# GpSimd for two of the four weight sums of gate and up's seven-product units, and a fourth such unit in ten groups

## The chip, the core and the metric

The kernel runs on one core of a Trainium2 chip. The core has five engines with queues of their own that run side by side and meet at semaphores: TensorE (PE in the profile) multiplies matrices, VectorE (DVE) and ScalarE (ACT) work element by element, GpSimd (POOL) can do that too and here mostly starts transfers, and SyncE (SP) only starts transfers. Each engine takes its own instructions strictly in order. TensorE writes its products to PSUM; all other tiles lie in SBUF. The metric is the time of one execution in microseconds; the median of several runs counts.

## What is computed

One layer of an encoder on 256 rows of 2048 columns, in float32: four mixers side by side, cross attention, and a gated MLP. Only the MLP is touched:

```python
def swiglu(h, w_gate_up, w_down):
    gate, up = jnp.split(h @ w_gate_up, 2, axis=-1)
    return (jax.nn.silu(gate) * up) @ w_down
...
        x = x + swiglu(rms_norm(x, norm_g[l, 2]), w_gate_up[l], w_down[l])
    return rms_norm(x, final_norm_g)
```

`w_gate_up` is 2048 x 11264, `w_down` 5632 x 2048.

## The kernel before

**Products of split numbers.** TensorE multiplies in a rounded format (`fp32r`). To keep float32's accuracy each operand is split into a high part (the number, rounded) and a low part (what is left). One product of 128 rows by 128 columns by 512 columns then takes three matmuls: high times high, high times low, low times high (`part`, L493 to L498). For weights the split is made in the kernel: ScalarE casts a piece of a slab to `wh` (L156), and VectorE subtracts, `wl = raw - wh` (L157).

**The stream of weights.** All weights come in the order of use from one array `W`, in slabs of 128 x 2048 (1 MB each). `Stream.raw` starts a slab's load on SP's queue (L136) as soon as one of its three buffers is free; in gate and up a fourth buffer serves every fourth slab. `Stream.make` splits the next piece into a pair `wh`, `wl`; in gate and up there are five such pairs of buffers, so the splitting engines can be at most five pieces ahead of TensorE. A pair is free again when TensorE has used it.

**Gate and up.** `Block.gate_up` goes through 11 groups `j` of 512 columns of gate and the same 512 columns of up. A group has eight slabs `i`; slab `i` holds rows 2i and 2i+1 (in tiles of 128) of both column blocks, four blocks of 128 x 512. The 256 rows of the activations are two halves, so a slab is a product of 2 x 2 blocks with 2 x 2 blocks:

- A plain slab takes eight products. It has two pieces of 1024 columns, each of which serves four products.
- A seven-product unit forms sums of blocks and takes seven products (Strassen's scheme in Winograd's form). `sevens(j)` says which slabs are units: 5 in group 0, and 1, 3 and 5 in groups 1 to 10. The sums of the activations are the same for all groups and are formed once, by `left()`, in group 0.

A unit's four weight blocks lie in the slab as b11, b12, b22, b21. `make` goes through it in four parts. Part 0 splits b11 alone (512 columns), and then one instruction of 1024 columns overwrites b11 and b12 by b11 - b12 and b22 - b12. Part 1 splits b22 and b21 as they are, and then two instructions of 512 columns each overwrite them: b22 becomes b22 + (b11 - b12), and b21 becomes b21 minus that. Part 2 splits the first two sums, part 3 the last two. Part 0 serves one product, the other three parts two each. `keep` fixes the order of these instructions on each engine as it is written.

After a group `combine` puts the unit products together, `finish` adds the plain ones, applies SiLU and the product, and `store_turned` transposes the result in blocks of 32 on VectorE and writes it to `hidden` in memory with eight transfers a group from GpSimd's queue. `fetch` reads parts of `hidden` back into `tmp` (L941), for the first sixteen tiles while gate and up still run, for the rest in down. `turn` writes the residual, transposed, to memory and reads it back (L1077, L1081), also on GpSimd's queue, spread over the first groups.

**Down** follows with the same stream and some units of its own (slabs from `DOWN` on). It works on the transposed `hidden`.

Of the kernel before, what the change touches and what calls it, by code (L numbers as in the profile page):

```python
# [18 lines left out]
ALU = mybir.AluOpType  # L19
# [3 lines left out]
P = 128  # L23
# [28 lines left out]

def sevens(j):

    return (1, 3, 5) if j else (5,)


FORMED = 6
# [20 lines left out]
DOWN = GU // 16 + 16 * DFF // 1024  # L79
# [6 lines left out]
def seven(slab):  # L86

    j, i = divmod(slab - GU // 16, 8)
    return slab in UNITS if slab >= DOWN else j >= 0 and i in sevens(j)
# [22 lines left out]
class Stream:  # L112
# [48 lines left out]
    def make(self):  # L161

        nc, (slab, part) = self.nc, self.todo
        n = 16 * slab + 8 * part
        if n >= NBLK - HELD:
            parts = [(self.places.pop(0)) for _ in range(2)]
            r = self.raw(slab)[:, part * 1024:part * 1024 + 1024]
            for a, (wh, wl) in zip((0, 512), parts):
                nc.scalar.copy(wh, r[:, a:a + 512])
                nc.vector.tensor_tensor(out=wl, in0=r[:, a:a + 512], in1=wh.bitcast(F32), op=ALU.subtract)  # L170
            self.bg.dve(1024, 2)
            self.items.append((None, parts))
            self.todo = (slab + part, 1 - part)
            return True
        pool = self.free(slab)
        if pool is None:
            return False
        raw = self.raw(slab)
        at = 48 if any(a <= n < b for a, b in ROWS) else 8
        r = raw[:, part % 2 * 1024:part % 2 * 1024 + 1024]  # L180
        if not seven(slab):
            mark = len(nc.cur_bb.bb.instructions)
            self.split(pool, at, r, [0, 256, 512, 1024] if n == 0 else [0, 512, 1024] if n == 8 else [0, 1024])
            if DOWN <= slab < DOWN + 2 * AHEAD:
                self.keep(mark)
            self.todo = (slab + part, 1 - part)
            return True
        mark = len(nc.cur_bb.bb.instructions)
        op = lambda out, a, b, what=ALU.subtract: nc.vector.tensor_tensor(out=out, in0=a, in1=b, op=what)  # L189
        self.split(pool, at, r, [0, 512] if part == 0 else [0, 1024])  # L190
        b11, b12, b22, b21 = (raw[:, a:a + 512] for a in range(0, 2048, 512))
        if part == 0:
            blk = raw.rearrange("p (b c) -> p b c", b=4)
            op(r.rearrange("p (b c) -> p b c", b=2), blk[:, 0:3:2, :], blk[:, 1:2, :].to_broadcast([P, 2, 512]))
            self.bg.dve(1024)
        elif part == 1:
            op(b22, b22, b11, ALU.add)
            op(b21, b21, b22)
            self.bg.dve(1024, 2)
        self.keep(mark)  # L200
        self.todo = (slab + part // 3, (part + 1) % 4)
        return True
# [87 lines left out]
class Block:  # L290
# [226 lines left out]
                    self.bg.poll()  # L517
        return ps

    def store_turned(self, to, u, src, keep=False):  # L520

        nc = self.nc
        self.bg.dve(src.shape[1])
        mark = self.mark()
        nc.vector.transpose(u, src)  # L525
        if keep:
            self.keep_place(mark)
        to = to.rearrange("(b f) t -> f b t", f=32)
        for a in range(4):
            nc.gpsimd.dma_start(to[:, :, 32 * a:32 * a + 32],  # L530
                                u[32 * a:32 * a + 32, :].rearrange("f (b t) -> f b t", t=32))


# [238 lines left out]
    def attention(self):  # L772
        tc, nc, act, st = self.tc, self.nc, self.act, self.st
        with tc.tile_pool(name="atp", bufs=1) as atp, tc.tile_pool(name="kp", bufs=1) as kp, \
# [24 lines left out]
            def load_kv():  # L799
# [12 lines left out]
                for _ in range(5):  # L812
                    fetch()
# [118 lines left out]
    def fetch(self, f, ks, ahead, pause, form=None):  # L932

        m = {}
        for n in range(len(ks) + ahead):
            if n < len(ks):
                k = ks[n]
                while len(self.stored) <= k // 4:
                    yield
                m[k] = self.tmp()  # L940
                self.nc.gpsimd.dma_start(m[k], self.ff[k * P:(k + 1) * P, :])  # L941
            if n >= ahead:
                i = ks[n - ahead]
                if i >= PLAIN:
                    if i % 2:
                        form(i - 1, m.pop(i - 1), m.pop(i))
                        self.have += 2
                        yield 3.0
                    continue
                mark = self.mark()  # L950
                self.split(f[i], m.pop(i))
                self.keep_place(mark)
                self.have += 1
                yield pause

    def gate_up(self, sw, gp, f):

        nc, st = self.nc, self.st
# [6 lines left out]

        def left():

            for i in (5, 1, 3):
                t = [self.tmp() for _ in range(2)]
                for x, k in zip(t, (2 * i, 2 * i + 1)):  # L970
                    nc.scalar.activation(x, self.resk(k), AF.Copy, scale=self.gvec(V_NG + 32, k))
                (a11, a21), (a12, a22) = ((x[:, 0:P], x[:, P:R]) for x in t)
                s = gp.tile([P, 512], F32, name="u", tag="u", bufs=2)
                s1, s2, s3, s4 = (s[:, a:a + P] for a in range(0, 512, P))
                self.stt(s1, a21, -1.0, a22, ALU.mult, ALU.subtract)
                self.stt(s2, s1, -1.0, a11, ALU.mult, ALU.subtract)
                self.tt(s3, a11, a21, ALU.subtract)
                self.tt(s4, a12, s2, ALU.subtract)
                yield
                h, l = sums[i] = [sw.tile([P, 512], F32R, name=f"s{x}{i}") for x in "hl"]  # L980
                self.split2(h, l, s)
                yield
# [26 lines left out]
        def finish(j, cs, s):  # L1009

            for r in range(2):
                self.tt(s[r][0], cs[r][0], s[r][0], ALU.add)
                nc.scalar.activation(s[r][0], s[r][0], AF.Silu, scale=box["col"][:, r:r + 1])
                yield SOON
            for r in range(2):
                g, h = s[r]
                self.tt(h, cs[r][1], h, ALU.add)
                yield SOON
            for r in range(2):
                g, h = s[r]  # L1020
                u = gp.tile([P, 512], F32, name="u", tag="u", bufs=2)
                self.stt(h, h, box["col"][:, r:r + 1], g, ALU.mult, ALU.mult)
                yield SOON
                self.store_turned(self.ff[j * 512:(j + 1) * 512, r * P:(r + 1) * P], u, h)
                yield SOON
            self.stored.append(j)

        ready = [self.late, self.bg.add(norm())]
        forms = self.bg.add(left())
        turned = self.bg.add(self.turn())  # L1030
        early = end = None
        for j in range(DFF // 512):
# [5 lines left out]
            for i in range(8):  # L1038
# [18 lines left out]
                for k in (2 * i, 2 * i + 1):  # L1057
                    for c in range(2):
                        wh, wl = st.take("w_gate_up", k, cols[c], 4)
                        for r in range(2):  # L1060
                            self.part_rows(cs[r][c], r, self.h3[k], wh, wl, k == 0, k == KT - 1)
                            self.bg.poll()
            self.bg.drain(last)
            end = self.bg.add(finish(j, cs, s))
        return end, turned, early

    def turn(self):

        nc = self.nc
        to = self.xr.rearrange("(b t) f -> t b f", t=32)  # L1070
        for i in range(16):
            u = self.tmp()
            self.bg.dve(R)
            nc.vector.transpose(u, self.resk(i))
            for a in range(4):
                c = i * P + 32 * a
                nc.gpsimd.dma_start(to[:, :, c:c + 32], u[32 * a:32 * a + 32, :].rearrange("t (b f) -> t b f", f=32))  # L1077
            yield 4.0
        for c in range(4):
            for r in range(2):  # L1080
                nc.gpsimd.dma_start(self.half(c, r), self.xr[r * P:(r + 1) * P, c * 512:(c + 1) * 512])  # L1081
            yield

    def half(self, c, r):
# [4 lines left out]
class Down:  # L1089
# [8 lines left out]
    def form(self, k, m1, m2):  # L1098


        b = self.b
        (a11, a21), (a12, a22) = ((x[:, 0:P], x[:, P:R]) for x in (m1, m2))
        s = self.sd.tile([P, 512], F32, name="e", tag="e", bufs=4)[:, 0:384]
        s2, s3, s4 = (s[:, a:a + P] for a in range(0, 384, P))
        b.tt(s3, a11, a21, ALU.subtract)
        b.stt(a21, a21, -1.0, a22, ALU.mult, ALU.subtract)
        b.stt(s2, a21, -1.0, a11, ALU.mult, ALU.subtract)
        b.tt(s4, a12, s2, ALU.subtract)
        b.split(self.f[k], m1)
        b.split(self.f[k + 1], m2)  # L1110
        t = self.sd.tile([P, 768], F32R, name=f"s{k}")
        b.split2(t[:, 0:384], t[:, 384:768], s)
        self.forms[k] = t
# [765 lines left out]
```

## Time and profile before

| | us |
|---|---|
| median of three runs (1453.46 to 1453.94) | 1453.75 |
| the run that was profiled | 1454.31 |
| its span, first to last instruction | 1452.4 |
| gate and up on TensorE, first to last matmul (749.6 to 1207.6) | 458.0 |
| sums of weight blocks on VectorE (L189), x129, first and last start | 768.7 and 1388.2 |
| loads of weights L136, x259, issue time of one on SP | 0.33 |
| stores of hidden L530, x88, issue time of one on GpSimd | 0.65 |

The granted clock of TensorE was 0.998. The page gives busy times of each engine and, in forty slices of the span, busy tenths. A row of instructions names line, engine, operation and tiles, then busy time, count or mean, and behind the bar the idle time in front of them with the engine that ended it. In a view in order of time a row gives the start, the length, the instruction and, in brackets, the idle time before it and what ended that. A row of a stretch gives each engine's busy time in it. The rows themselves stand in the prediction where they are used.

### The profile page before, as it was taken

The numbers are of one execution on the slowest core, as the hardware profiler recorded it, in microseconds if no ns is written. First come the engines' busy times: TensorE is split into PE (matmuls) and PEld (weight loads), VectorE is DVE, ScalarE is ACT, GpSimd is POOL, SyncE is SP. The second block draws the span as 40 slices with busy tenths as digits, with TensorE's granted clock in tenths as the row PEclk, the third lists the DMA queues.
The fourth block names the chain that finished last, engine by engine and source line by source line (L and its number), as shares of the span: only waits on it lengthen the run. The fifth ranks groups of instructions, "written<-read, shape, count | busy, mean of one in ns | idle before, by whom it ended". The sixth has DMA issues, their size and how long they took to land.

```text
span 1452.4 us, 19765 instructions
## 1 busy us (share of the span) xinstructions
PE 1439.1 (99%) x7231; PEld 1217.8 (84%) x7231; DVE 1192.3 (82%) x1750; ACT 844.1 (58%) x1254; POOL 172.2 (12%) x294
## 2 busy tenths in 40 slices
PE   9999999999999999999999999999999999999997
PEld 8888888898899888888888888888888888788886
DVE  6587768778868767877778999999999997988875
ACT  6565655466656646765565555555655564655554
POOL 0220100000000001100003334112111112100000
PEclk9999999999999999999999999999999999999999
DMA  9985654454535656555555767666667656655654
GB/s 352 339 289 197 220 193 168 152 187 156 195 129 206 215 179 224 172 170 195 178 205 205 277 234 243 220 209 237 233 220 250 221 200 220 214 184 199 225 203 146
DMA packets 57394, 307.17 MB, mean 211 GB/s; under 512 B 9773, under 2 KB 11470, under 8 KB 25680
## 3 DMA queue, kind: packets, MB, share of 16 engines
q1 hardware_dynamic: 45920, 281.11, 54.9%
q0 software_dynamic: 10944, 24.14, 5.4%
q8 instruction: 57, 0.93, 0.3%
q10 hardware_dynamic: 432, 0.66, 0.1%
q14 instruction: 41, 0.34, 0.1%
HBM read 291.71 MB, written 14.16 MB: 211 GB/s over the span
## 4 chain that ended last, share of the span: by engine, by line
PE 94%; DVE 2%; issue 2%; ACT 1%; DMA 1%; POOL 1%; SPq 0%; DVEq 0%; POOLq 0%; ACTq 0%
PE pg L444 19%; PE pg L496 13%; PE pg L497 13%; PE pg L495 13%; PE pg L445 10%; PE pm L496 6%; PE pm L495 6%; PE pm L497 6%; PE pm L1380 1%; DVE wl L157 1%; PE pg L441 1%; PE pg L442 1%; PE pm L895 1%; PE pm L868 1%; DMA tmp<-hidden 1%
## 5 line engine op out<-in xcount | busy, mean ns | idle before, releaser
L156 ACT CAST wh<-raw 128x1024 fp32r<-128x1024 f32 (+1 forms) x589 | 589.2, 1013 | 466.6 <-PE pg L497 149.7
L157 DVE TENSOR_TENSOR wl<-raw,wh 128x1024 fp32r<-128x1024 f32 (+1 forms) x589 | 681.4, 1175 | 177.8 <-ACT wh L156 171.7
L444 PE MATMUL pg<-act,wh 128*128 128x512 f32 x1104 | 387.5, 393 | 0.0
L445 PE MATMUL pg<-act,wl 128*128 128x256 f32 x1216 | 340.7, 280 | 0.0
L496 PE MATMUL pg<-wl,act 128*128 128x512 f32 (+1 forms) x689 | 268.3, 389 | 1.5 <-DVE wl L157 1.4
L495 PE MATMUL pg<-wh,act 128*128 128x512 f32 (+1 forms) x689 | 268.7, 391 | 0.0
L497 PE MATMUL pg<-wh,act 128*128 128x512 f32 (+1 forms) x689 | 268.3, 389 | 0.0
L444 PEld LDWEIGHTS pg<-act,wh 128*128 128x128 f32 x1104 | 207.4, 188 | 44.9
L445 PEld LDWEIGHTS pg<-act,wl 128*128 128x128 f32 x1216 | 228.5, 188 | 0.8 <-DVE wl L157 0.5
L496 PEld LDWEIGHTS pg<-wl,act 128*128 128x128 f32 x689 | 129.5, 188 | 29.6 <-DVE wl L157 3.1
L495 PEld LDWEIGHTS pg<-wh,act 128*128 128x128 f32 x689 | 129.6, 188 | 27.5 <-issue 0.8
L497 PEld LDWEIGHTS pg<-wh,act 128*128 128x128 f32 x689 | 129.4, 188 | 27.4 <-issue 0.4
L496 PE MATMUL pm<-wl,act 128*128 128x512 f32 x318 | 123.7, 389 | 0.0
L497 PE MATMUL pm<-wh,act 128*128 128x512 f32 x318 | 123.7, 389 | 0.0
L495 PE MATMUL pm<-wh,act 128*128 128x512 f32 x318 | 123.6, 389 | 0.0
L189 DVE TENSOR_TENSOR raw<-raw 128x1024 f32<-128x1024 f32 x129 | 111.7, 866 | 3.0
L530 POOL DMA_DIRECT2D hidden<-u x88 | 56.8, 653 | 162.3 <-DVE u L525 139.7
L495 PEld LDWEIGHTS pm<-wh,act 128*128 128x128 f32 x318 | 59.7, 188 | 12.5
L497 PEld LDWEIGHTS pm<-wh,act 128*128 128x128 f32 x318 | 59.7, 188 | 12.4
L496 PEld LDWEIGHTS pm<-wl,act 128*128 128x128 f32 x318 | 59.7, 188 | 12.4
L1077 POOL DMA_DIRECT2D xrows<-tmp x64 | 37.0, 586 | 182.7 <-DVE rc L323 126.6
L941 POOL DMA_DIRECT2D tmp<-hidden x44 | 24.5, 560 | 145.7 <-DVE f L319 73.4
(361 smaller groups left out, 1778.6 us busy)
## 6 DMA issues: line engine op xcount, KB each, us to landing
raw<-in_W SPq DMA_DIRECT2D x246, 1024.0 KB, 5.0
raw<-in_W SPq DMA_DIRECT2D x11, 512.0 KB, 7.5
hidden<-u POOLq DMA_DIRECT2D x88, 64.0 KB, 4.4
tmp<-hidden POOLq DMA_DIRECT2D x44, 128.0 KB, 4.6
res<-in_xT SPq DMA_DIRECT2D x8, 512.0 KB, 8.4
k<-in_mem SPq DMA_DIRECT2D x8, 256.0 KB, 6.8
k<-in_x SPq DMA_DIRECT2D x8, 256.0 KB, 9.9
keys<-k POOLq DMA_DIRECT2D x32, 64.0 KB, 5.4
```

What stands on the lines that cost most here:

```text
L156: nc.scalar.copy(wh[:, a:b], r[:, a:b])
L157: nc.vector.tensor_tensor(out=wl[:, a:b], in0=r[:, a:b], in1=wh[:, a:b].bitcast(F32), op=ALU.subtract)
L189: op = lambda out, a, b, what=ALU.subtract: nc.vector.tensor_tensor(out=out, in0=a, in1=b, op=what)
L441: self.nc.tensor.matmul(p[:, 0:R], wh, slot[:, 0:R], start=start, stop=False)
L444: self.nc.tensor.matmul(p[:, :], wh, slot[:, :], start=start, stop=False)
L445: self.nc.tensor.matmul(p[:, 0:R], wl, slot[:, 0:R], start=False, stop=stop)
L495: self.nc.tensor.matmul(p, hi, wh, start=start, stop=False)
L496: self.nc.tensor.matmul(p, hi, wl, start=False, stop=False)
L497: self.nc.tensor.matmul(p, lo, wh, start=False, stop=stop)
L530: nc.gpsimd.dma_start(to[:, :, 32 * a:32 * a + 32], u[32 * a:32 * a + 32, :].rearrange("f (b t) -> f b t", t=32))
L941: self.nc.gpsimd.dma_start(m[k], self.ff[k * P:(k + 1) * P, :])
L1077: nc.gpsimd.dma_start(to[:, :, c:c + 32], u[32 * a:32 * a + 32, :].rearrange("t (b f) -> t b f", f=32))
```

## The change

Three things change, all in gate and up:

1. `sevens` adds slab 4: in groups 1 to 10 slabs 1, 3, 4 and 5 are units, so three of them follow each other. `left()` forms the sums of the activations for it too.
2. In part 1 of a unit of gate and up the two sums of 512 columns are made by GpSimd in place of VectorE. Down's units keep them on VectorE. The tally of VectorE's work by which small tasks are spaced leaves them out.
3. The stores of `hidden`, the early loads of `tmp` and the whole of `turn` start from SP's queue, where the weight loads are, in place of GpSimd's. The loads of `tmp` in down, with `form`, stay on GpSimd.

```diff
 def sevens(j):
-    return (1, 3, 5) if j else (5,)
+    return (1, 3, 4, 5) if j else (5,)
...
         elif part == 1:
-            op(b22, b22, b11, ALU.add)
-            op(b21, b21, b22)
-            self.bg.dve(1024, 2)
+            if slab < DOWN:
+                nc.gpsimd.tensor_tensor(out=b22, in0=b22, in1=b11, op=ALU.add)
+                nc.gpsimd.tensor_tensor(out=b21, in0=b21, in1=b22, op=ALU.subtract)
+            else:
+                op(b22, b22, b11, ALU.add)
+                op(b21, b21, b22)
+                self.bg.dve(1024, 2)
...
-    def store_turned(self, to, u, src, keep=False):
+    def store_turned(self, to, u, src, keep=False, queue=None):
...
-            nc.gpsimd.dma_start(to[:, :, 32 * a:32 * a + 32],
+            (queue or nc.gpsimd).dma_start(to[:, :, 32 * a:32 * a + 32],
...
-                self.nc.gpsimd.dma_start(m[k], self.ff[k * P:(k + 1) * P, :])
+                (self.nc.gpsimd if form else self.nc.sync).dma_start(m[k], self.ff[k * P:(k + 1) * P, :])
...
-            for i in (5, 1, 3):
+            for i in (5, 1, 3, 4):
...
-                self.store_turned(self.ff[j * 512:(j + 1) * 512, r * P:(r + 1) * P], u, h)
+                self.store_turned(self.ff[j * 512:(j + 1) * 512, r * P:(r + 1) * P], u, h, queue=nc.sync)
...
-                nc.gpsimd.dma_start(to[:, :, c:c + 32], u[32 * a:32 * a + 32, :].rearrange("t (b f) -> t b f", f=32))
+                nc.sync.dma_start(to[:, :, c:c + 32], u[32 * a:32 * a + 32, :].rearrange("t (b f) -> t b f", f=32))
...
-                nc.gpsimd.dma_start(self.half(c, r), self.xr[r * P:(r + 1) * P, c * 512:(c + 1) * 512])
+                nc.sync.dma_start(self.half(c, r), self.xr[r * P:(r + 1) * P, c * 512:(c + 1) * 512])
```

## Prediction

> **What bounds the kernel now.** I read the page's busy shares first, then the busy times over stretches as long as one group of gate and up, then the order of time inside a unit on VectorE, ScalarE and TensorE, and last the rows that come nearest to the new GpSimd work. "Unit" is a slab multiplied with seven products, "plain" one with eight.
>
> ```profile
> span 1452.4 us, 19765 instructions
> PE 1439.1 (99%) x7231; PEld 1217.8 (84%) x7231; DVE 1192.3 (82%) x1750; ACT 844.1 (58%) x1254; POOL 172.2 (12%) x294
> DVE  6587768778868767877778999999999997988875
> ```
>
> TensorE works all the time, VectorE 82% over the span but nine tenths or more from the 23rd slice to the 33rd, which is gate and up. The ten whole groups that get a fourth unit, a stretch each:
>
> ```profile
> core 0: us, PE busy (x) PEld busy (x) DVE busy (x) ACT busy (x) POOL busy (x), PEclk, DMA share, GB/s
> 793.00:834.50 41.50, 41.50 (x184) 34.35 (x183) 39.91 (x48) 23.96 (x27) 13.15 (x22) 1.00 0.69 239
> ...
> 1166.30:1207.60 41.30, 41.30 (x184) 34.17 (x183) 38.93 (x46) 24.20 (x28) 6.32 (x10) 1.00 0.58 198
> sum 414.60, PE 414.60 PEld 343.28 DVE 394.73 ACT 235.86 POOL 92.28; mean PE 41.46 PEld 34.33 DVE 39.47 ACT 23.59 POOL 9.23
> ```
>
> TensorE sets each group's 41.46 us, and VectorE is busy for 39.47 of them: 2.0 us to spare. One unit of the last group, in order of time on the three engines (start, us, instruction):
>
> ```profile
> 1187.48 1.22 DVE L189 TENSOR_TENSOR raw<-raw 128x1024 f32<-128x1024 f32 x1
> 1188.63 1.22 DVE L157 TENSOR_TENSOR wl<-raw,wh 128x1024 fp32r<-128x1024 f32 x1
> 1189.88 1.42 DVE L189 TENSOR_TENSOR raw<-raw 128x512 f32<-128x512 f32 x2
> 1191.21 0.42 DVE L319 TENSOR_TENSOR f<-tmp,f 128x256 fp32r<-128x256 f32 x1
> 1191.55 8.03 DVE L157 TENSOR_TENSOR wl<-raw,wh 128x1024 fp32r<-128x1024 f32 x7
> ...
> 1188.82 1.05 ACT L156 CAST wh<-raw 128x1024 fp32r<-128x1024 f32 x1 [1.82 <-DVE raw L189]
> 1191.41 3.02 ACT L156 CAST wh<-raw 128x1024 fp32r<-128x1024 f32 x3 [1.54 <-DVE raw L189]
> ...
> 1192.87 0.39 PE L495 MATMUL pg<-wh,sh 128*128 128x512 f32 x1
> ...
> 1195.59 0.39 PE L495 MATMUL pm<-wh,sh 128*128 128x512 f32 x1
> ```
>
> The two sums are the third line (1189.88 to 1191.30). The unit's last cast follows at 1191.41, 0.11 us behind them: it already waits for the sums. The `wl` run after them takes 8.03/7 = 1.15 us for one; its second, the unit's last, ends near 1193.85, and TensorE first wants it at 1195.59. So a unit's last part is ready 1.7 us ahead. Between the two TensorE lines lie twelve matmuls: 0.227 us for one, 0.68 for a product of three.
>
> **The change, part by part, for one group (1 to 10).**
>
> *The fourth unit* takes one product away: −0.68 us on TensorE, 40.78 us a group. Were nothing else to change, that is 10 × −0.68 = −6.8 us.
>
> *VectorE's work.* Three units give up two sums each, 6 × 1.42/2 = −4.3 us. A unit in place of a plain slab adds one `wl` of 1024 (1.15), one of 512 (0.69) and the double sum (1.15):
>
> ```profile
> L189 DVE TENSOR_TENSOR raw<-raw 128x512 f32<-128x512 f32 x36 | 24.8, 688 | 0.7
> L157 DVE TENSOR_TENSOR wl<-raw,wh 128x512 fp32r<-128x512 f32 x18 | 12.3, 685 | 0.3 <-ACT wh L156 0.3
> ```
>
> Together +3.0, so 39.47 − 4.3 + 3.0 = 38.2 us of work in 40.78: 2.6 us to spare, as long as VectorE never waits. The fourth unit's sums of activations are formed once, in group 0, which has one unit; they hide in that group's spare time, some 2 us if they did not.
>
> *The wait that comes instead.* In a unit the steps after the second `wl` were sum, sum, third `wl`, fourth `wl`, all on VectorE with the casts beside them. Now both sums go to GpSimd, which cannot start before the second `wl` has read the block, and the last cast waits for GpSimd. Queued behind that cast on ScalarE are the next slab's casts; behind the fourth `wl` on VectorE the next slab's `wl`s; and TensorE waits for both. The changed program's order leaves VectorE nothing but the third `wl` to do meanwhile in the second, third and fourth unit of a group (a split of hidden or a transpose stands there now and then); only in the first do five sums of the group before stand in between.
>
> What a GpSimd sum costs is not in this trace. The nearest rows:
>
> ```profile
> L1580 POOL MEMSET gs<- 128x512 f32 x2 | 1.0, 526 | 123.8 <-DVE res L319 123.8
> masks.py:199 POOL TENSOR_SCALAR_AFFINE_SELECT ident<-ident 128x128 f32<-128x128 f32 x1 | 0.3, 287 | 0.1
> ```
>
> Below: 0.53 us, a fill of the same size that reads nothing. Above: 2 × 4 × 0.287 = 2.3 us, if each of two inputs costs what the one input of the second row does at a quarter of the size. I take 4 × 0.287 = 1.15 us, the only row that reads SBUF.
>
> The chain from the end of the second `wl` to the start of the fourth is then two sums 2.3, the cast 1.05, and three hand-overs at 0.11 (as above) 0.3: 3.65 us. The third `wl` (1.15) either runs beside the sums, which leaves VectorE idle for 2.5 us, or it and the sums exclude each other, which leaves 3.65. No row has VectorE and GpSimd reading SBUF together, so I take the middle, 3.05, and keep both ends. In the first unit the five sums (5 × 0.69 = 3.4 us) and the third `wl` cover 4.6 us: idle 0, or about 1.0 at the serial end.
>
> Idle of VectorE over its spare time becomes time of the group, since five buffers of weights (four products of 0.68 us each in a plain part, 13.6 us at the most) can't carry a deficit that comes back every group: 3 × 3.05 − 2.6 = +6.5; against before, with −0.68, **+5.9 us a group, +59 us in ten**. With the ends of the overlap: 3 × 2.5 − 3.28 = +4.2 (+42) and 3 × 3.65 + 1.0 − 3.28 = +8.7 (+87). With a sum at 0.53 and overlap the idle time is 1.26: 3.8 − 3.28 = +0.5 (+5). With a sum at 2.3, overlapped, the idle time is 4.8: +11.1 (+111).
>
> On GpSimd itself nine of down's loads of `tmp` now stand, in four places, ahead of sums of groups 9 and 10, and hold them up where they wait for a buffer:
>
> ```profile
> POOL tmp L941 <- DVE f L319: 73.4, 13, 12.7
> ```
>
> 5.6 us a wait here, so at most 4 × 5.6 = +22 us; I take 0, since they were placed where a buffer should be free, and keep the end for the range.
>
> *Transfers on SP's queue.* All that gate and up issues besides weights (88 stores of hidden, 64 of rows, 16 loads, 8 of the residual) now stands among the weight loads.
>
> ```profile
> L136 SPq DMA_DIRECT2D raw<-in_W x259: 327/328/801, 1.2 to 1421.6; - x130
> raw<-in_W SPq DMA_DIRECT2D x246, 1024.0 KB, 5.0
> L530 POOL DMA_DIRECT2D hidden<-u x88 | 56.8, 653 | 162.3 <-DVE u L525 139.7
> hidden<-u POOLq DMA_DIRECT2D x88, 64.0 KB, 4.4
> SPq L136 <- DVE wl L157: 805.4, 160, 13.3
> ```
>
> SP mostly waits for a free buffer (last line), so issue time alone is covered: eight stores at 0.33 to 0.65 us are 2.6 to 5.2 us a group. In the order of the changed program the weight loads in front of a group's stores run to the fourth, fifth or sixth slab of the next group, while VectorE makes `u` in its second: three to four slabs, over 20 us, for stores and one load (5.2 + 5.0). Only group 1 has a slab less. I put it at 0, from 0 to +15 us. GpSimd loses its queue of stores ahead of the `tmp` loads at the end of the stage; TensorE's idle time there bounds what that can bring, to −2.9 us:
>
> ```profile
> 1240.00:1280.00 40.00, 37.07 (x160) 29.37 (x159) 36.71 (x65) 23.25 (x37) 3.80 (x7) 1.00 0.62 223
> ```
>
> **Sum.** Span 1452.4 + 59 = 1511.4. The run that was profiled took 1454.31, 1.9 more than its span; the median of the runs, 1453.75, is 1.35 more. 1511.4 + 1.4 = **1513 us**.
>
> **The rivals.**
>
> *VectorE and GpSimd take turns at SBUF* (the serial end): +87, **1541 us**. For it: nearly all of VectorE's work here, `wl<-raw,wh` above all, has two inputs from SBUF, and so have the sums. Against: no row shows it. The Trainium skill, SBUF — State Buffer, section "Who interferes with whom", states just this: a VectorE instruction with two SBUF inputs contends with a GpSimd one that reads SBUF, and the loser blocks for the whole instruction. By that rule the time would be the 1541 that the rows give; no run so far shows it. It would make `wl` rows of 2 us and more, or GpSimd sums well over their time alone.
>
> *It fits* (the other side): the fourth part's wait ends before VectorE has run out of other work, TensorE keeps its pace and the products saved are all that is left: 1453.75 − 6.8 = **1447 us**. It decides at 3 s below 2.6 us, so an idle time s under 0.87 a unit; 2 T + 1.35 − 1.15 < 0.87 asks for a sum T under 0.34 us. A fill alone takes 0.53, which speaks against it; for it speaks only that the five buffers can be full when a group's first unit comes.
>
> *SP's queue becomes the wait*: stores wait for `u`, the weight load behind them for the stores, and if each waits in addition for the landing of a store (4.4 us) the load lands 5.2 + 4.4 + 5.0 = 14.6 us after `u`. Where one slab of lead is missing that is about 4 us late; in four groups +15, **1528 us**. For it: SP becomes one line for both kinds. Against: the lead above.
>
> *The sums are quick* (0.53 us): +5, **1459 us**; TensorE waits a little in each group.
>
> **How the numbers follow.** Forecast 0.45, turns at SBUF 0.33, SP's queue 0.10, it fits 0.07, quick sums 0.05. What a measurement can tell from no change is about 0.2%, 2.9 us: faster 0.07; the same 0.03, from the quick end of the quick sums; slower 0.90. The range leaves out "it fits", the quick sums and a slice of the serial end with dearer sums: 1470 to 1560.
>
> **What would show it.** Right: GpSimd sums of 128x512 near 1.15 us, ScalarE's cast waiting for GpSimd once a unit, TensorE waiting for `wl` in the third to fifth slab of each group, groups of some 47 us, VectorE busy less of a group than before. Serial: groups near 50 us, and `wl` rows or sums stretched where they overlap. Wrong: TensorE busy for the whole group at 40.8 us; or its waits ending on weight loads, not on VectorE.

## The result and the profile after

The changed kernel takes 1554.16 us (1552.08 to 1556.49, four runs) against 1453.85 us before: 1.069 times as long, 95% interval 1.0676 to 1.0703. The profiled execution's span went from 1452.4 to 1553.1 us, so 100.7 us are to be found.

The ten groups with four units, the first, the second and the last of them, as busy times in a stretch each (the sum is over all ten):

```profile
core 0: us, PE busy (x) PEld busy (x) DVE busy (x) ACT busy (x) POOL busy (x), PEclk, DMA share, GB/s
793.80:842.10 48.30, 43.91 (x181) 34.57 (x180) 38.19 (x42) 24.90 (x29) 12.43 (x8) 0.96 0.46 136
842.10:897.10 55.00, 46.57 (x182) 35.47 (x181) 43.52 (x47) 24.68 (x28) 15.11 (x8) 0.94 0.61 202
...
1255.40:1306.50 51.10, 44.08 (x180) 34.20 (x180) 40.17 (x45) 25.74 (x30) 16.29 (x10) 0.97 0.51 168
sum 512.70, PE 450.30 PEld 349.92 DVE 400.99 ACT 247.92 POOL 143.61; mean PE 45.03 PEld 34.99 DVE 40.10 ACT 24.79 POOL 14.36
```

They take 512.7 us where the ten took 414.6: 51.3 us a group for 41.5, +98.1 of the 100.7. Each group has about three matmuls fewer, and TensorE stands still for 6.2 us of it (51.27 − 45.03). VectorE is busy for 40.1 of 51.3 us: it isn't the bound by its work, it waits.

One unit of group 9, the third engine now beside VectorE and ScalarE:

```profile
1226.86 2.50 DVE L157 TENSOR_TENSOR wl<-raw,wh 128x1024 fp32r<-128x1024 f32 x2
1232.97 1.22 DVE L157 TENSOR_TENSOR wl<-raw,wh 128x1024 fp32r<-128x1024 f32 x1 [3.61 <-ACT wh L156]
...
1231.89 1.04 ACT L156 CAST wh<-raw 128x1024 fp32r<-128x1024 f32 x1 [3.79 <-POOL raw L199]
...
1228.16 2.36 POOL L198 TENSOR_TENSOR raw<-raw 128x512 f32<-128x512 f32 x1 [5.41 <-DVE wl L157]
1230.59 1.27 POOL L199 TENSOR_TENSOR raw<-raw 128x512 f32<-128x512 f32 x1
...
1228.13 0.50 PE L500 MATMUL pm<-wl,sh 128*128 128x512 f32 x1 [0.63 <-DVE wl L157]
1232.99 0.51 PE L499 MATMUL pg<-wh,sh 128*128 128x512 f32 x1 [2.03 <-ACT wh L156]
1234.25 0.50 PE L500 MATMUL pg<-wl,sh 128*128 128x512 f32 x1 [0.75 <-DVE wl L157]
```

Read it as a chain. The first DVE line is the unit's second and third `wl`; it ends at 1229.36. GpSimd's first sum starts at 1228.16, once the second `wl` is done, but takes 2.36 us; the second sum takes 1.27. Then come the cast and at 1232.97 the fourth `wl`. VectorE has stood still for 3.61 us, and TensorE waits for the cast and then for the `wl`. The first sum is longer than the second by 1.1 us: by the time for which the third `wl` runs beside it. Over the whole kernel:

```profile
L198 POOL TENSOR_TENSOR raw<-raw x41: 1282/2347/2358, 772.6 to 1288.2; 128x512 f32<-128x512 f32 x41
...
L199 POOL TENSOR_TENSOR raw<-raw x41: 1262/1290/2252, 774.4 to 1290.6; 128x512 f32<-128x512 f32 x41
...
L157 DVE TENSOR_TENSOR wl<-raw,wh x609: 417/1222/2352, 4.5 to 1526.7; 128x1024 fp32r<-128x1024 f32 x151, 128x256 fp32r<-128x256 f32 x1, 128x512 fp32r<-128x512 f32 x1
```

(Shortest, median, longest in ns.) The `wl` before:

```profile
L157 DVE TENSOR_TENSOR wl<-raw,wh x589: 416/1219/1229, 4.7 to 1425.7; 128x1024 fp32r<-128x1024 f32 x185, 128x512 fp32r<-128x512 f32 x11, 128x256 fp32r<-128x256 f32 x1
```

A sum alone takes 1.28 us. Where a sum and a `wl` run at the same time, one of the two takes about 1 us longer, mostly the sum, sometimes the `wl` (up to 2352 ns, and never over 1229 before). The wait of 3.6 us is not in every unit: VectorE has it in 19 of the 20 second and third units of groups 1 to 10, in three of the ten fourth ones and in none of the first.

### The profile page after: what moved, and what is told of

Its sections match the earlier page's. It is cut to its first block, busy times and chain, and to the rows that moved or that the text cites. A ratio compares the mean times of both kernels' runs of the same rounds, so it can differ in the third digit from the quotient of the medians.

```text
span 1553.1 us, 19814 instructions
## 1 busy us (share of the span) xinstructions
PE 1476.0 (95%) x7201; PEld 1224.3 (79%) x7201; DVE 1199.0 (77%) x1723; ACT 858.0 (55%) x1277; POOL 206.2 (13%) x200
## 4 chain that ended last, share of the span: by engine, by line
PE 67%; DVE 13%; POOL 7%; issue 7%; ACT 4%; DMA 2%; SPq 0%; POOLq 0%; DVEq 0%; ACTq 0%
PE pg L448 17%; PE pg L449 9%; PE pg L500 9%; PE pg L501 9%; PE pg L499 9%; DVE wl L157 8%; POOL raw L198 4%; ACT wh L156 3%; POOL raw L199 3%; PE pm L500 3%; PE pm L501 3%; PE pm L499 2%; DVE raw L189 2%; DMA raw<-in_W 1%; PE pm L1384 1%
## 5 line engine op out<-in xcount | busy, mean ns | idle before, releaser
L157 DVE TENSOR_TENSOR wl<-raw,wh 128x1024 fp32r<-128x1024 f32 (+1 forms) x609 | 713.5, 1189 | 278.9 <-ACT wh L156 272.0
L156 ACT CAST wh<-raw 128x1024 fp32r<-128x1024 f32 (+1 forms) x609 | 601.0, 1006 | 543.1 <-PE pg L501 134.4
L500 PE MATMUL pg<-wl,act 128*128 128x512 f32 (+1 forms) x664 | 261.0, 393 | 4.2 <-DVE wl L157 4.1
L499 PE MATMUL pg<-wh,act 128*128 128x512 f32 (+1 forms) x664 | 261.3, 397 | 1.1 <-ACT wh L156 1.1
L501 PE MATMUL pg<-wh,act 128*128 128x512 f32 (+1 forms) x664 | 260.6, 393 | 0.0
L499 PEld LDWEIGHTS pg<-wh,act 128*128 128x128 f32 x664 | 126.6, 191 | 30.1 <-ACT wh L156 3.2
L198 POOL TENSOR_TENSOR raw<-raw 128x512 f32<-128x512 f32 x41 | 81.7, 1993 | 495.5 <-DVE wl L157 338.9
L501 PEld LDWEIGHTS pg<-wh,act 128*128 128x128 f32 x664 | 126.0, 190 | 27.0 <-issue 0.4
L500 PE MATMUL pm<-wl,act 128*128 128x512 f32 x293 | 117.3, 400 | 0.5 <-DVE wl L157 0.5
L499 PE MATMUL pm<-wh,act 128*128 128x512 f32 x293 | 116.7, 402 | 0.2 <-ACT wh L156 0.2
L501 PE MATMUL pm<-wh,act 128*128 128x512 f32 x293 | 116.6, 399 | 0.0
L189 DVE TENSOR_TENSOR raw<-raw 128x1024 f32<-128x1024 f32 (+1 forms) x77 | 81.2, 1055 | 1.8
L199 POOL TENSOR_TENSOR raw<-raw 128x512 f32<-128x512 f32 x41 | 60.4, 1473 | 3.2
L499 PE MATMUL pm<-wh,sh 128*128 128x512 f32 x83 | 35.6, 431 | 18.5 <-ACT wh L156 18.4
```

The lines of the kernel that those rows point to most:

```text
L156: nc.scalar.copy(wh[:, a:b], r[:, a:b])
L157: nc.vector.tensor_tensor(out=wl[:, a:b], in0=r[:, a:b], in1=wh[:, a:b].bitcast(F32), op=ALU.subtract)
L198: nc.gpsimd.tensor_tensor(out=b22, in0=b22, in1=b11, op=ALU.add)
L199: nc.gpsimd.tensor_tensor(out=b21, in0=b21, in1=b22, op=ALU.subtract)
L499: self.nc.tensor.matmul(p, hi, wh, start=start, stop=False)
L500: self.nc.tensor.matmul(p, hi, wl, start=False, stop=False)
```

## The experiments

Twelve kernels ran. Six of them, with before and after, make a full table of the change's three parts; four take the GpSimd sums apart, and two the transfers. "Before" was between 1453.2 and 1454.4 us beside each of them.

**Parts of the change left out.** First the change without its fourth unit:

```diff
-    return (1, 3, 4, 5) if j else (5,)
+    return (1, 3, 5) if j else (5,)
```

> The change without its fourth unit: three units a group, their two sums on GpSimd, transfers on SP. Turn-taking (VectorE's subtractions and GpSimd's sums exclude each other): VectorE's work falls to 39.5 - 4.3 = 35.2 us of 41.46, 6.3 us to spare, and it idles 3.65 us in two units and about 1.0 in the first: +2.0 us a group, about 1474 us. Wait alone (third wl beside the sums, 2.75 us idle at a sum of 1.28): 5.5 us fit into 6.3, 1454 us. SP's queue as the cause: about 1454 + 15 whatever the sums do.

Measured: 1500.6 us, 27 more than turn-taking alone gives. The run with the transfers alone, the next but one, accounts for some 15 of them.

Then the change without GpSimd's sums:

```diff
-            if slab < DOWN:
-                nc.gpsimd.tensor_tensor(out=b22, in0=b22, in1=b11, op=ALU.add)
-                nc.gpsimd.tensor_tensor(out=b21, in0=b21, in1=b22, op=ALU.subtract)
-            else:
-                op(b22, b22, b11, ALU.add)
-                op(b21, b21, b22)
-                self.bg.dve(1024, 2)
+            op(b22, b22, b11, ALU.add)
+            op(b21, b21, b22)
+            self.bg.dve(1024, 2)
```

> The change without GpSimd's sums: four units a group, all sums on VectorE, transfers on SP. Both theories of the sums: VectorE's work is 39.47 + 1.42 + 3.0 = 43.9 us against 40.78 on TensorE, +3.1 - 0.68 = +2.4 us a group, about 1478 us. If the run of three units in a row is itself the trouble, with no lead left at the fifth slab, it would be nearer to the 1554 of the change.

Measured: 1492.7 us, 61.5 less than the change. So the three units in a row are not the main trouble; GpSimd's sums are. But it is also 15 above the 1478 that both theories gave, and the run of the fourth unit by itself, below, shows that this is not SP's queue.

Both edits together leave the transfers on SP as the only part of the change.

> Only the transfers on SP's queue; three units, sums on VectorE. Turn-taking and wait alone: within 3 us of 1453.8, perhaps 1 to 3 us less through the shorter queue of stores at the end of the stage. SP's queue as the cause of part of the 100 us: 1465 to 1470, with ScalarE's casts waiting for weight loads.

Measured: 1469.6 us, ratio 1.0103 (1.0088 to 1.0118). SP's queue by itself costs 15 us with three units, where the prediction had taken 0, with up to 15 in its range. SP's own order of time shows where:

```profile
868.40 0.33 SPq L136 DMA_DIRECT2D raw<-in_W  x1
878.44 1.80 SPq L1077 DMA_DIRECT2D xrows<-tmp  x4
882.09 8.12 SPq L530 DMA_DIRECT2D hidden<-u  x8
890.31 2.22 SPq L136 DMA_DIRECT2D raw<-in_W  x4
```

From 868.40 to 890.31 no load of weights starts: SP stands at a store of rows until VectorE has transposed them, then takes 8 us over the stores of hidden. ScalarE's casts wait 7.7 us for one of these loads.

Last, the change with its transfers left on GpSimd:

```diff
-                self.store_turned(self.ff[j * 512:(j + 1) * 512, r * P:(r + 1) * P], u, h, queue=nc.sync)
+                self.store_turned(self.ff[j * 512:(j + 1) * 512, r * P:(r + 1) * P], u, h)
...
-                nc.sync.dma_start(to[:, :, c:c + 32], u[32 * a:32 * a + 32, :].rearrange("t (b f) -> t b f", f=32))
+                nc.gpsimd.dma_start(to[:, :, c:c + 32], u[32 * a:32 * a + 32, :].rearrange("t (b f) -> t b f", f=32))
```

(and the loads of `tmp` and of the residual likewise)

> The change with all transfers left on GpSimd's queue, between the sums. Turn-taking: sums now also stand behind transfers that wait for VectorE's transposes: not below 1554, about 1560 to 1600 us. SP's queue as the cause: 1540 us or less.

Measured: 1542.5 us. Neither expectation fits. In the change, SP's queue costs 11.7 us more than GpSimd's does, whatever the sums lose there behind the transfers.

**Sums that nobody waits for.** In each unit of gate and up two sums of the same size on GpSimd, into a tile that is never read, beside VectorE's real ones; the transfers on SP, so 1469.6 us is what to compare with.

```diff
+            if slab < DOWN:
+                lo = self.items[-1][2].bitcast(F32)
+                for _ in range(2):
+                    nc.gpsimd.tensor_tensor(out=self.scratch, in0=lo[:, 0:512], in1=lo[:, 512:1024], op=ALU.add)
```

> Three units, the real sums on VectorE, transfers on SP, and beside them two sums of 128x512 on GpSimd in each unit of gate and up whose result nobody reads (they read the unit's second wl). No instruction waits for them but the next writer of that buffer. Turn-taking: 6 x 1.28 = 7.7 us a group in which VectorE or GpSimd stands still; at most 7.7 - 2.0 = +5.7 us a group, 1510 us; if half of the loss falls on GpSimd's side or beside work from PSUM, 1475. Wait alone: nobody waits, so 1454 us, and GpSimd's sums take 1.28 us each, VectorE's wl 1.22 us.

Measured: 1516.1 us, +46. The bound of 1510 was counted from 1453; from 1469.6 the same +5.7 us a group gives 1527. The trace has no instruction that waits for one of these sums, the next writer of the buffer that they read included, so this is the price of the two engines at SBUF alone. It shows on VectorE's own sums of 512 columns, 0.69 us before:

```profile
L189 DVE TENSOR_TENSOR raw<-raw 128x512 f32<-128x512 f32 x58 | 74.6, 1285 | 1.1
```

With one idle sum in place of two (`range(1)`):

> As the run with two idle GpSimd sums a unit (1516 us, 46 above the same kernel without them at 1469.6), with one. Turn-taking, each sum costing VectorE its 1.28 us once the spare time is used: between 18 (3 x 1.28 - 2.0 a group) and 23 us (half of 46) above 1469.6, so 1488 to 1493 us. If the loss came from something else that the idle sums bring (the moved tiles, the buffer that the sum holds): the same 1516, or 1470.

Measured: 1484.4 us, 14.8 above 1469.6. That is a little less than the 18 to 23 forecast, and neither 0 nor 46. The first sum of a unit costs 15 us and the second 32: the first partly falls into VectorE's spare time.

**Fills for sums.** The change with writes in place of the two sums (this kernel leaves the sums out):

```diff
-                nc.gpsimd.tensor_tensor(out=b22, in0=b22, in1=b11, op=ALU.add)
-                nc.gpsimd.tensor_tensor(out=b21, in0=b21, in1=b22, op=ALU.subtract)
+                for x in (b22, b21, b22, b21, b22):
+                    nc.gpsimd.memset(x, 0.0)
```

> The change with GpSimd's two sums left out: five fills of 128x512 write the two blocks in their place, about 2.5 us as two sums of 1.28 us take, so the chain and its waits are the same but GpSimd reads nothing. Turn-taking of reads: the third wl runs beside the fills, VectorE idles 2.75 us in three units: 3 x 2.75 - 2.6 - 0.68 = +5.0 us a group, about 1504 us. If GpSimd's writes exclude VectorE too: as the change, about 1554 us, with fills of more than 1 us where a wl runs.

Measured: 1487.6 us, 66.6 less than the change. Instructions of GpSimd, then of VectorE:

```profile
L199 POOL MEMSET raw<- x205: 514/519/546, 772.3 to 1224.7; 128x512 f32 x103
...
L157 DVE TENSOR_TENSOR wl<-raw,wh x609: 415/1221/1229, 4.8 to 1459.4; 128x1024 fp32r<-128x1024 f32 x151, 128x256 fp32r<-128x256 f32 x1, 128x512 fp32r<-128x512 f32 x1
```

No `wl` is over 1229 ns and no fill over 546. That they do run side by side shows in the second unit of group 1, VectorE and then GpSimd:

```profile
804.36 2.50 DVE L157 TENSOR_TENSOR wl<-raw,wh 128x1024 fp32r<-128x1024 f32 x2
809.14 1.83 DVE L157 TENSOR_TENSOR wl<-raw,wh 128x1024 fp32r<-128x1024 f32 x2 [2.29 <-ACT wh L156]
...
805.63 2.40 POOL L199 MEMSET raw<- 128x512 f32 x5 [9.69 <-DVE wl L157]
```

The five fills start with the third `wl` and take 2.40 us. VectorE still waits for the cast behind them, but 2.3 us and not 3.6, and in groups 1 to 9 only the second and third units have this wait; the forecast of 1504 had 2.75 us in three units. What VectorE is held up by is thus GpSimd's sums, which read SBUF, and not writes to the same blocks.

**Where VectorE reads PSUM.** The fourth unit with transfers on GpSimd, and GpSimd's sums in a group's first unit only, where VectorE has the additions of the group before:

```diff
-            if slab < DOWN:
+            if slab < DOWN and (slab - GU // 16) % 8 == 1:
```

> The fourth unit with transfers on GpSimd (1491.3 us with all sums on VectorE), and GpSimd makes the two sums of a group's first unit only, beside which VectorE has four or five additions with one input from PSUM. Turn-taking of two SBUF inputs alone: those additions run beside GpSimd, VectorE gives up 1.4 us a group and loses at most the 1.2 us of one wl: between 1477 and 1491 us, and GpSimd's sums near 1.3 us with the additions at 0.69. If any instruction of VectorE excludes GpSimd's: above 1491, with additions of more than 1 us.

Measured: 1490.9 us, the same as with all sums on VectorE (1491.3, below). One such unit, VectorE and then GpSimd:

```profile
1014.53 0.68 DVE L323 TENSOR_TENSOR h<-pg,g 128x512 f32<-128x512 f32 x1
1015.13 1.28 DVE L323 TENSOR_TENSOR g<-pm,g 128x512 f32<-128x512 f32 x2
1016.33 2.17 DVE L157 TENSOR_TENSOR wl<-raw,wh 128x1024 fp32r<-128x1024 f32 x1
...
1014.76 1.29 POOL L198 TENSOR_TENSOR raw<-raw 128x512 f32<-128x512 f32 x1 [4.38 <-DVE wl L157]
1016.13 1.29 POOL L199 TENSOR_TENSOR raw<-raw 128x512 f32<-128x512 f32 x1
```

The time alone decides nothing, since it lies where the two expectations meet; the rows do. The additions with one input from PSUM (`pg`, `pm`) take their 0.68 us, two of them 1.28, beside the first sum. The `wl` that starts while the second sum runs takes 2.17 us in place of 1.22: from the end of the sum, 1017.42, to its own, 1018.50, it is 1.08. GpSimd took 1.4 us of work over, and the `wl` lost 0.95 of it again here; the rest may be the longer chain.

**The rest of the table.** Only the fourth unit:

> Only the fourth unit: sums on VectorE, transfers on GpSimd. VectorE's work 43.9 us against 40.8 on TensorE: +2.4 us a group, 1478 us; from the run of four units with all transfers on SP (1492.7) less the 15 us of SP: 1477.

Measured: 1491.3 us, +38 and not +24. From the start of group 1 to that of group 10, before and here:

```profile
793.00:1166.30 373.30, 373.30 (x1648) 309.11 (x1647) 355.80 (x411) 211.67 (x238) 85.95 (x141) 1.00 0.66 231
```

```profile
792.80:1195.90 403.10, 380.57 (x1622) 300.16 (x1621) 390.29 (x450) 222.27 (x253) 87.02 (x143) 1.00 0.62 211
```

A group takes 403.1/9 = 44.8 us for 41.5, and VectorE is busy for 43.4 of them, near the 43.9 of the forecast. The 1.4 us in which it still stands idle were not in the forecast; 0.9 of them are waits for casts (8.2 us in the nine groups). That the casts can't run ahead because they wait for the unit's sums themselves is a likely reason, not a tested one. These nine groups make 30 of the 38 us; the others come in the last group or behind it.

Only GpSimd's sums, three units and transfers on GpSimd:

> Only the sums on GpSimd: three units, transfers on GpSimd. With SP's part (12 to 15 us) taken off the run that has them on SP (1500.6): 1486 to 1488 us. Turn-taking as first worked out (two units at 3.65 us idle, 1.0 in the first, 6.3 us to spare): 1474. Wait alone: 1454. If sums that queue behind transfers on GpSimd cost more than SP's order does: above 1500.

Measured: 1478.3 us, +25. Turn-taking as first worked out, 1474, comes nearest; the estimate by way of SP's part is 8 us or more too high.

The two halves of the transfers, with three units and all sums on VectorE:

> Of the transfers only the residual's (64 stores of rows, 8 loads back) on SP; three units, sums on VectorE. In the run with all transfers on SP one weight load was started 22 us after the one ahead of it, behind four stores of rows that waited for VectorE's transpose and eight stores of hidden. If the stores of rows are the cause: most of the 15 us, about 1463 to 1470 us. If the stores of hidden are: within 3 us of 1453.8.

Measured: 1453.8 us, ratio 1.0002 (0.9993 to 1.0011). The stores of rows alone cost nothing.

> The other half: the stores of hidden and the early loads of tmp on SP, the residual's on GpSimd. If the stores of rows are the cause of the 15 us: 1454 to 1458 us. If the stores of hidden are: 1463 to 1470 us. If it takes both together, each half alone stays under 1460.

Measured: 1457.1 us, ratio 1.0025 (1.0015 to 1.0036). It takes both kinds in the one queue: 0 and 3.6 us alone, 15 together. With hidden alone SP starts four loads of weights between 867.95 and 886.09, where with both it stood still.

The table, medians in us:

| | transfers on GpSimd | transfers on SP |
|---|---|---|
| three units, sums on VectorE | 1453.9 (before) | 1469.6 |
| three units, sums on GpSimd | 1478.3 | 1500.6 |
| four units, sums on VectorE | 1491.3 | 1492.7 |
| four units, sums on GpSimd | 1542.5 | 1554.2 (the change) |

Each of the three parts costs time by itself, and no version with any of them is faster than before. The sums on GpSimd cost 24 us with three units and 51 with four (transfers on GpSimd); SP's queue costs 16, 22, 1 and 12 us from row to row, which no run explains.

## Why the prediction was right or wrong

The direction was right and the time lies inside the range, at its far side: forecast +59 us, measured +100. Point by point:

- *The product saved*, 0.68 us a group: right as a count (about 181 matmuls a group for 184) and worth nothing, since TensorE waits 6.2 us a group.
- *VectorE's work in four units*, 38.2 us: the profile has 40.1, of which 201 `wl` at 1279 in place of 1216 ns make 12.7 us in ten groups, 1.3 a group; that is blocked time, not work. Within 0.6 us right.
- *The chain from the second `wl` to the fourth*: at the serial end 3.65 + 1.15 = 4.8 us; measured 1228.08 to 1232.97, 4.89 us. Its parts: a sum 1.28 us (taken 1.15), the cast 1.04 (1.05).
- *The step that failed in size is the overlap of the third `wl` with the sums.* It was taken half way, 3.05 us of idle time, between 2.5 (side by side) and 3.65 (taking turns). The chip takes turns: 3.61 us idle in the unit shown. That is the rival of the prediction with 0.33, which made 1541 us of it; the change without SP's transfers, where that sum belongs, takes 1542.5. That it comes so near is partly luck, since two errors cancel. A sum costs 1.28 us and not 1.15, which makes 2 × 0.13 us more in each of four units, about 10 us in all. Against that, the full wait was reckoned in three units of a group, and it is there in two of them and in few of the fourth ones. The 1.0 us of the first unit had no working behind it.
- *The rule of the Trainium skill*, SBUF — State Buffer, section "Who interferes with whom", which stood beside that rival: the runs agree with all three of its parts that bear on this kernel. Two inputs from SBUF beside a GpSimd instruction that reads SBUF: the later one waits until the other is done (2.36 for 1.28 us, 2.17 for 1.22). A GpSimd instruction that only writes: no effect (`wl` at most 1229 ns). One input from SBUF, the other from PSUM: no effect (0.68 us). The trace of before has no row that could have shown it. The middle that was taken between the two cases is not what either of them would give.
- *Transfers on SP's queue at 0, from 0 to +15*: 11.7 us in the change. The working looked at when the stores of hidden come and left out the stores of rows in front of them; with three units it takes both, the rows waiting for VectorE's transposes and then the hidden, to make a load late. What the 11.7 us are in the change itself is not settled: the casts' waits for weights are 11.5 us there and 13.3 us with the transfers on GpSimd, so they don't show the difference, which spreads over the groups (51.3 us against 50.4 for one on average).
- *Loads of `tmp` ahead of sums at 0*: no wait of a sum goes back to them, and groups 9 and 10 took 50.8 and 51.1 us, like the others. Right.
- *The end of the stage*, at best −2.9: nothing came. From the last matmul of gate and up to the end of the span it is 244.8 us before and 246.6 after.
- *It fits* needed a sum under 0.34 us, and *the sums are quick* one of 0.53; it takes 1.28. With a sum at 2.3 us the working left out 1.35 us of idle time in the first unit (5.95 − 4.6); it changes nothing here.

With the serial end and SP's measured share the sum of the prediction would be 1541 + 11.7 = 1553, with the same two errors in it.

## What to carry to other kernels

Before element-wise work moves from VectorE to GpSimd, look at what VectorE does beside it. Where its instructions have two inputs in SBUF, as here, they and GpSimd's sums take turns (1.28 us for a sum that cost VectorE 0.69); here VectorE's additions with an input in PSUM ran on. A saving on the engine that sets the pace is no saving when the helper that feeds it has less to spare than it costs: 0.68 us of TensorE for 4.4 us of VectorE with 2.0 to spare made +38 us. Transfers that wait for other engines can hold up the queue that keeps the weights coming, and two kinds that cost 0 and 3.6 us each cost 15 together.

## What was not expected of the hardware

In the change, where TensorE waits, its granted clock was lower: 0.998 before, 0.981 after, with 0.90 in groups 5 and 6.

```profile
998.70:1049.60 50.90, 46.29 (x182) 36.13 (x181) 40.65 (x44) 24.89 (x29) 12.42 (x9) 0.90 0.57 197
1049.60:1100.70 51.10, 46.21 (x181) 36.16 (x180) 39.89 (x43) 24.77 (x29) 12.44 (x9) 0.90 0.62 205
1204.60:1255.40 50.80, 44.14 (x181) 34.54 (x180) 40.48 (x43) 25.01 (x29) 18.42 (x16) 0.97 0.62 210
```

No cost of it shows: TensorE was busy 2 us longer in the two groups at 0.90 than in the third line's at 0.97, and the groups took the same time. Waiting alone does not bring it about either: with the fourth unit alone TensorE stood still for 22.5 us in nine groups, and the clock of that stretch is 1.00 in the row above. What makes the difference was not tested.
